# A mixer of four attentions: the memory pairs run in steps inside the stick-breaking pairs

## The chip, the cores and the metric

The kernel runs on one core of a Trainium2 chip. The metric is the time of one execution on the device, in microseconds. The median of three runs of the kernel before is 3154.68 us (3153.85 to 3159.28).

## What is computed

Two layers work on 2048 tokens of width 1024. Each layer projects its input once and feeds four groups of four heads of width 64: `fox` (causal softmax with a learned decay), `sb` (stick-breaking), `mla` (causal softmax on compressed keys and queries) and `mem` (softmax over 256 memory rows). Each group's output is multiplied by a gate, an output projection follows, and a layer norm over a scaled residual ends the layer.

```python
proj = jnp.einsum('bsd,dc->bsc', h_res, w_in[l])
# stick-breaking, for each query block; valid is key < query
z = jnp.einsum('bhqd,bhkd->bhqk', qb, k) * scale
log_keep = jnp.where(valid, jax.nn.log_sigmoid(-z), 0.0)
log_tail = lax.cumsum(log_keep, axis=3, reverse=True) - log_keep
w = jnp.where(valid, jnp.exp(jax.nn.log_sigmoid(z) + log_tail), 0.0)
out = jnp.einsum('bhqk,bhkd->bhqd', w, v)
# memory
mem_p = jax.nn.softmax(jnp.einsum('bhsd,bhmd->bhsm', mq, mk) * head_scale, axis=-1)
out_mem = jnp.einsum('bhsm,bhmd->bhsd', mem_p, mv)
# all four groups
mixed = jnp.concatenate([out_fox, out_sb, out_mla, out_mem], axis=-1)
y = jnp.einsum('bsc,cd->bsd', mixed * jax.nn.silu(gate), w_out[l])
h_res = layer_norm(DEEPNORM_ALPHA * h_res + y, ln_g[l], ln_b[l])
```

## The kernel before

Every operand of a matmul is held as two float16 numbers, a high part and the rest (`split`, `hl_tile`), and each product is three matmuls (`mm3`). Heads go in pairs: two heads fill the 128 partitions. Tokens go in four chunks of 512.

A layer runs the groups of `PLAN` one after the other: the latent projections of `mla`, then `fox0`, `fox1`, `mla0`, `mla1`, `sb0`, `sb1`, and at the end `mem0` and `mem1` together, a chunk of the one and a chunk of the other by turns. Each pair is a Python generator (`pair`). Its first part loads and splits four weight matrices (`wprep`: 8 loads, 8 maxima on VectorE, 8 casts on ScalarE, 8 splits on VectorE, line 147). A memory pair also computes its keys and values here, once. Then it yields after each of the four chunks.

A chunk of a pair first projects keys, queries, values and the gate, then works head by head. In a stick-breaking pair the work of a head comes in groups of two query tiles of 128 (`g`) and blocks of 1024 keys (`b`), last block first. One tile of a block (`stick_tile`) takes scores on TensorE (line 332), two sigmoids on ScalarE (400, 401), a backward cumulative product on VectorE (the scan, 403), a one-column scaling and a product on GpSimd (404, 405), a cast on ScalarE (411), a subtraction on VectorE (412), a transposing DMA into `pt` (354) and the matmuls with the values (859). In a memory pair a head of a chunk is one block: scores for 512 queries and 256 rows (803), maxima and a tiny scaling on VectorE (807, 808), exponentials (811), a cast (814), a subtraction on GpSimd (815), a transposing DMA and four matmuls (820). When both heads are done, `half_sum` (451, 452) gathers the halves, and an epilogue multiplies by the gate and stores (`norm_gate` with line 445, `emit_g` with 456 and 461). The epilogue of a chunk is put on the list `pending` and run by `flush` after the gate of the next chunk.

The softmax pairs (`fox`, `mla`) write logits with VectorE (369, 371), subtract on GpSimd (389) and transpose by DMA. The output projection (937) holds 8 weight tiles: four in the two `pt` tiles and four in granules; each 128-token tile `yt` is a granule too.

The order of the work comes from a list scheduler. It takes instructions in the order in which the program traces them as their priority, lets a later one go first where the earlier is not ready or has no buffer, and fixes the order of each engine's queue. All DMAs go through SP's one queue. Buffers are counted: a granule (`sbp`, 4 KB a partition, 10 of them) holds a tile of scores, of the forget rows, of `kr`, of `craw`, of `yt`, and a memory block's `pe` and `pt`; a weight place (`wp`, 4 KB, 5 of them) holds one split weight matrix. There are two `q`, two `sg`, three `hl`, five key and five value tiles.

## Time and profile before

| | |
|---|---|
| median of the runs | 3154.68 us |
| the profiled execution's own time | 3160.48 us |
| its span, first to last instruction | 3158.5 us |
| busy: TensorE, VectorE, ScalarE, GpSimd | 81%, 72%, 61%, 49% |
| mean granted TensorE clock | 0.91 |
| stick-breaking stage of layer 0, from first scan to last subtraction | 861.6 to 1306.4 us |
| output projection of layer 0 | 1443.6 to 1614.1 us |

PE is TensorE, PEld its weight loads, DVE VectorE, ACT ScalarE, POOL GpSimd, SP the engine that issues the DMAs. A duration in the trace runs from the start to the end of an instruction on its engine, so it holds what the instruction waits for once it has begun. Idle time of an engine is put down to what ended it.

### The profile page before, as it was taken

Reading aid. Unit: us, or ns where it says so; the run is one execution under the profiler, and the core shown is the slowest. Engines: PE = TensorE matmul, PEld = TensorE weight load, DVE = VectorE, ACT = ScalarE, POOL = GpSimd, SP = SyncE. Lnnn points to the kernel's source line nnn. Section 1 sums busy time; section 2 is a strip of 40 time slices with the busy share of each in tenths; the row PEclk is TensorE's granted clock in tenths of the full one; section 3 lists DMA queues with packets and bytes.
Section 4 is the critical chain, followed back from the end, with each engine's and each line's share of the span. In section 5 each row is a group of like instructions: output and inputs, shape, how many; then the busy total and the mean of one; then the engine's idle time right before and its main releaser. Section 6 shows DMA issues by size and latency. Waiting matters only on the chain. (4 is left out here: it accounts for less than half of the span.)

```text
span 3158.5 us, 47091 instructions
## 1 busy us (share of the span) xinstructions
PE 2557.1 (81%) x16412; PEld 1374.9 (44%) x16412; DVE 2280.7 (72%) x4377; ACT 1913.3 (61%) x3543; POOL 1561.7 (49%) x1079
## 2 busy tenths in 40 slices
PE   2589897888986784798978899878889768659898
PEld 2345453444553442444434545444445435334443
DVE  7756767867679989757655475577676998994565
ACT  3447667877766676474234566677767766755600
POOL 5305545555678687443210246455657867772400
PEclk9889998999998897799989999999989889769999
DMA  7748978888755745657845478897977475465752
GB/s 190 196 126 167 191 154 188 176 174 174 150 103 115 155 87 112 139 119 191 235 116 126 90 162 163 165 189 157 176 157 135 91 168 101 96 148 114 170 181 100
DMA packets 1225038, 469.46 MB, mean 149 GB/s; under 512 B 1040304, under 2 KB 1184944, under 8 KB 1224656
## 3 DMA queue, kind: packets, MB, share of 16 engines
q1 hardware_dynamic: 1224800, 466.46, 67.8%
q8 instruction: 128, 2.10, 0.3%
q14 instruction: 110, 0.90, 0.1%
HBM read 141.07 MB, written 50.53 MB: 61 GB/s over the span
## 5 line engine op out<-in xcount | busy, mean ns | idle before, releaser
L389 POOL TENSOR_TENSOR hl<-sb,hl 128x1024 f16<-128x1024 f32 (+7 forms) x384 | 609.1, 1599 | 686.3 <-ACT hl L388 503.9
L332 PE MATMUL s<-k,q 128*128 128x512 f16 (+3 forms) x1920 | 529.4, 378 | 117.7 <-ACT sg L401 34.0
L859 PE MATMUL o<-pt,v 128*128 128x256 f16 (+3 forms) x3456 | 429.4, 299 | 200.3 <-DMA pt<-hl 194.8
L405 POOL TENSOR_TENSOR sg<-sg,kp 128x127 f32<-128x127 f32 (+3 forms) x192 | 384.4, 2004 | 119.7 <-DVE kp L403 95.3
L381 ACT ACTIVATE sb<-sb,sm,sc_all 128x1024 f32<-128x1024 f32 (+7 forms) x384 | 376.5, 981 | 76.0 <-DVE sm L377 75.4
L859 PEld LDWEIGHTS <-v 128*64 128x64 f16 (+1 forms) x3456 | 245.0, 112 | 401.7 <-DMA pt<-hl 201.3
L388 ACT CAST hl<-sb 128x1024 f16<-128x1024 f32 (+7 forms) x384 | 297.7, 791 | 184.2 <-DMA pt<-hl 174.0
L937 PE MATMUL s<-wo,gc 128*128 128x512 f16 x1536 | 335.2, 381 | 0.4 <-DVE yt L941 0.4
L332 PEld LDWEIGHTS <-q 128*128 128x128 f16 x1920 | 185.2, 104 | 321.0 <-issue 201.8
L412 DVE TENSOR_TENSOR hl<-sg,hl 128x128 f16<-128x128 f32 (+3 forms) x192 | 241.9, 1267 | 44.0 <-ACT hl L411 43.0
L411 ACT CAST hl<-sg 128x128 f16<-128x128 f32 (+3 forms) x192 | 152.9, 798 | 177.5 <-DMA pt<-hl 104.4
L369 DVE CUSTOM_DVE_ANT_0 sb<-s,fb 128x512 f32<-128x512 f32 (+2 forms) x320 | 184.3, 607 | 102.9 <-DMA fb<-fds 39.6
L371 DVE TENSOR_SCALAR_CACHE_REDUCE sb<-s 128x512 f32<-128x512 f32 (+2 forms) x320 | 185.5, 606 | 72.1 <-POOL hl L389 39.8
L937 PEld LDWEIGHTS <-gc 128*128 128x128 f16 x1536 | 150.9, 98 | 182.2 <-issue 3.9
L401 ACT ACTIVATE sg<-s,sc_all 128x512 f32<-128x512 f32 (+2 forms) x320 | 199.6, 629 | 40.4 <-POOL sg L405 22.1
L403 DVE TENSOR_TENSOR_SCAN kp<-kp 128x384 f32<-128x384 f32 (+7 forms) x128 | 216.6, 1705 | 8.8 <-ACT kp L400 7.7
L400 ACT ACTIVATE kp<-s,sc_all 128x512 f32<-128x512 f32 (+2 forms) x320 | 200.0, 627 | 29.0 <-PE s L332 9.4
L276 PE MATMUL pv<-w,hT 128*128 128x128 f16 x1024 | 191.6, 227 | 24.6 <-DVE k L286 24.6
L456 POOL TENSOR_TENSOR og<-og,sg 128x512 f32<-128x512 f32 x64 | 99.2, 1550 | 223.2 <-DVE og L452 124.0
L276 PE MATMUL pg<-hT,w 128*128 128x512 f16 x512 | 197.0, 385 | 8.1 <-DVE sb L371 3.7
L277 PE MATMUL pg<-hT,w 128*128 128x512 f16 x512 | 196.3, 383 | 0.0
L278 PE MATMUL pg<-hT,w 128*128 128x512 f16 x512 | 195.9, 383 | 0.0
(238 smaller groups left out, 5930.1 us busy)
## 6 DMA issues: line engine op xcount, KB each, us to landing
raw<-in_w_in_dram SPq DMA_DIRECT2D x100, 256.0 KB, 4.7
q<-q SPq DMA_DIRECT2D x128, 128.0 KB, 2.8
fb<-fds SPq DMA_DIRECT2D x32, 512.0 KB, 4.0
gd<-gh SPq DMA_DIRECT2D x128, 128.0 KB, 2.6
raw<-in_w_out_dram SPq DMA_DIRECT2D x64, 256.0 KB, 3.8
gc<-gd SPq DMA_DIRECT2D x64, 256.0 KB, 4.0
yt<-ah SPq DMA_DIRECT2D x32, 512.0 KB, 5.3
raw<-ctd SPq DMA_DIRECT2D x48, 256.0 KB, 3.1
```

Source lines behind the costliest of these rows:

```text
L276: T.matmul(ps, lh, rh, start=(first and k == 0), stop=False)
L332: T.matmul(ps[:, :m], qs[:, h, v, j * P:(j + 1) * P], ks[c][:, h, :m], start=(v == 0), stop=last)
L381: A.activation(t, t, AF.Exp, scale=sc, bias=sm[:, j, 2:3], accum_out=su[:, b, col + j:col + j + 1])
L388: A.copy(hi, t)
L389: G.tensor_tensor(lo, t, hi, op=ALU.subtract)
L400: A.activation(keep[:, o:o + m], ps[:, :m], AF.Sigmoid, scale=nsc)
L401: A.activation(w[:, o:o + m], ps[:, :m], AF.Sigmoid, scale=sc)
L403: V.tensor_tensor_scan(keep[:, ::-1], keep[:, ::-1], keep[:, ::-1], cy, op0=ALU.mult, op1=ALU.bypass)
L405: G.tensor_tensor(w[:, :n - 1], w[:, :n - 1], keep[:, 1:n], op=ALU.mult)
L412: V.tensor_tensor(lo, w, hi, op=ALU.subtract)
L859: T.matmul(o[r0:r1, oc + j0 * P:oc + 256], vs[k // 4][:, k % 4, h, 0:r1 - r0], pcol(pt, a, k % 8, kb, j0), start=(n == 1), stop=(n == total))
L937: T.matmul(ps, gc[a][k // 4][:, k % 4, t * P:(t + 1) * P], wo[k][:, b2, n * 512:(n + 1) * 512], start=(k == 0 and a == 0 and b2 == 0), sto ...
```

## The change

`PLAN` merges each memory pair with a stick-breaking pair: `['mem0', 'sb0']`, then `['mem1', 'sb1']`. Generators now yield more often: after the gate of a chunk, after each head of a memory chunk, after each block of 1024 keys of the other kinds. `TURNS` gives the order in the merged groups: 1 is a step of the stick-breaking pair, 0 one of the memory pair. A stick-breaking chunk has 5, 5, 9 and 9 steps, a memory chunk 3. So the first two stick-breaking chunks run alone (ten steps), the third has four memory steps among it and the last has eight. Groups of one pair run through as before. Chunks of `mem` and `sb` flush their epilogue at once.

Space is moved: one more weight place, one granule less, two `og` tiles for one, one `kf` for two, and fewer small tiles under the tags of `smp`.

```diff
-PLAN = [['lat'], ['fox0'], ['fox1'], ['mla0'], ['mla1'], ['sb0'], ['sb1'], ['mem0', 'mem1']]
+PLAN = [['lat'], ['fox0'], ['fox1'], ['mla0'], ['mla1'], ['mem0', 'sb0'], ['mem1', 'sb1']]
+
+TURNS = {'mem': [1] * 10 + [1, 1, 1, 0] + [1, 1, 0] * 3 + [1] + [1, 0] * 8}
...
-    wp = pool("wp", 5)
+    wp = pool("wp", 6)
     ptp = pool("ptp", 2)
-    sbp = pool("sbp", 10)
+    sbp = pool("sbp", 9)
...
-                kf = op.tile([P, 4, 36], F32, name=nm("kf"), tag="kf", bufs=2)
+                kf = op.tile([P, 4, 36], F32, name=nm("kf"), tag="kf", bufs=1)
...
                     sg = gate_tanh(wg, u2, c, hops(c))
+                yield
 
                 flush()
-                og = op.tile([P, 512], F32, name=nm("og"), tag="og")
+                og = op.tile([P, 512], F32, name=nm("og"), tag="og", bufs=2)
...
                         half_sum(o, og, h)
+                        yield
                         continue
...
-                    half_sum(o, og, h)
+                            if (g, b) == (2 * c + 1, bs[-1]):
+                                half_sum(o, og, h)
+                            yield
...
                 pending.append(epilogue)
-                yield
+                if kind in ("mem", "sb"):
+                    flush()
...
             gens, coming = coming, None
-            for c in range(NCH):
-                if norm:
+
+            if norm:
+                for _ in range(NCH):
                     next(norm, None)
-                if c == AHEAD[gi] and gi + 1 < len(PLAN):
-                    coming = start(gi + 1)
-                for g in gens:
-                    next(g)
+                    next(gens[0])
+            turns = TURNS.get(PLAN[gi][0][:-1])
+            for g in turns or []:
+                next(gens[g], None)
+            for g in gens:
+                for _ in g:
+                    pass
```

In `smp`, the tags `am`, `at`, `ad`, `gb`, `ry`, `rt`, `mv` go from 4 tiles to 2, `wt` from 4 to 2, `sm` from 8 to 6, `cy` from 8 to 4.

## Rows read from the trace of the kernel before

**Rows 1.** Part 1 of the page: busy us (share of span) of each engine.
```profile
PE 2557.1 (81%) x16412; PEld 1374.9 (44%) x16412; DVE 2280.7 (72%) x4377; ACT 1913.3 (61%) x3543; POOL 1561.7 (49%) x1079
```

**Rows 2.** Stretches: length, then busy us of PE, PEld, DVE, ACT, POOL, clock.
```profile
862.00:1308.00 446.00, 319.66 (x2240) 179.25 (x2239) 405.97 (x410) 295.54 (x514) 335.72 (x219) 0.84 0.60 119
...
1308.00:1444.00 136.00, 122.95 (x673) 62.30 (x672) 78.50 (x154) 88.54 (x207) 47.22 (x34) 0.94 0.57 127
...
2402.00:2843.00 441.00, 322.30 (x2246) 181.78 (x2245) 406.25 (x412) 296.25 (x515) 331.81 (x219) 0.84 0.59 120
```

**Rows 3.** Stick-breaking lines, by source line: ns min/median/max, first and last start.
```profile
L403 DVE TENSOR_TENSOR_SCAN kp<-kp x64: 399/1504/3787, 861.6 to 1283.7; 128x128 f32<-128x128 f32 x8, 128x256 f32<-128x256 f32 x8, 128x384 f32<-128x384 f32 x8, 128x512 f32<-128x512 f32 x8
...
L403 DVE TENSOR_TENSOR_SCAN kp<-kp,cy x32: 2327/2345/2754, 936.4 to 1293.5; 128x1024 f32<-128x1024 f32 x32
...
L412 DVE TENSOR_TENSOR hl<-sg,hl x96: 279/1202/3044, 875.1 to 1306.4; 128x1024 f16<-128x1024 f32 x40, 128x128 f16<-128x128 f32 x8, 128x256 f16<-128x256 f32 x8, 128x384 f16<-128x384 f32 x8
...
L404 POOL TENSOR_SCALAR sg<-sg x64: 182/622/2164, 861.6 to 1284.2; 128x1 f32<-128x1 f32 x64
...
L403 DVE TENSOR_TENSOR_SCAN kp<-kp x64: 400/1504/3683, 2401.6 to 2819.9; 128x128 f32<-128x128 f32 x8, 128x256 f32<-128x256 f32 x8, 128x384 f32<-128x384 f32 x8, 128x512 f32<-128x512 f32 x8
```

**Rows 4.** Timeline of POOL and DVE from 1223: start, us, engine, line.
```profile
1223.73 6.28 POOL L405 TENSOR_TENSOR sg<-sg,kp 128x1023 f32<-128x1023 f32 x1 [2.22 <-DVE kp L403]
...
1230.21 1.99 POOL L405 TENSOR_TENSOR sg<-sg,kp 128x1023 f32<-128x1023 f32 x1
...
1228.24 1.78 DVE L121 TENSOR_SCALAR sc_all<-sc_all 128x2 f32<-128x2 f32 x1
...
1230.31 3.78 DVE L403 TENSOR_TENSOR_SCAN kp<-kp 128x896 f32<-128x896 f32 x1
```

**Rows 5.** Lines of the memory stage, layer 0: count, busy us, mean ns.
```profile
L815 POOL TENSOR_TENSOR hl<-pe,hl 128x1024 f16<-128x1024 f32 x16 | 34.0, 2128 | 47.5 <-ACT hl L814 47.4
...
L461 POOL TENSOR_TENSOR gh<-og,gh 128x256 f16<-128x256 f32 x16 | 10.7, 671 | 20.1 <-ACT gh L460 20.1
...
L456 POOL TENSOR_TENSOR og<-og,sg 128x512 f32<-128x512 f32 x8 | 10.6, 1326 | 40.5 <-DVE sg L445 35.0 <-DVE og L452 2.8 <-DVE smm L808 2.8
...
L807 DVE TENSOR_REDUCE smm<-s 128x2 f32<-128x512 f32 x32 | 21.4, 686 | 14.6 <-PE s L803 14.5
...
L286 DVE SCALAR_TENSOR_TENSOR q<-pq,q 64x512 f16<-64x512 f32 x16 | 11.0, 689 | 6.6 <-ACT q L285 6.2
...
L452 DVE TENSOR_TENSOR og<-o,og 64x512 f32<-64x512 f32 x16 | 11.0, 687 | 9.4 <-ACT og L451 9.2
...
L808 DVE TENSOR_SCALAR smm<-smm,sc_all 128x2 f32<-128x2 f32 x32 | 10.8, 344 | 0.5
...
L445 DVE TENSOR_TENSOR sg<-sg,rb 128x512 f32<-128x512 f32 x8 | 5.5, 685 | 1.1 <-PE rb L444 0.9
...
L431 DVE SCALAR_TENSOR_TENSOR sg<-sg,pg 128x512 f32<-128x512 f32 x8 | 5.5, 683 | 6.2 <-ACT sg L430 6.2
```

**Rows 6.** The memory scalings of both layers, by source line, columns as rows 3.
```profile
L808 DVE TENSOR_SCALAR smm<-smm,sc_all x64: 210/224/1678, 1335.5 to 2978.0; 128x2 f32<-128x2 f32 x64
```

**Rows 7.** The output projection's matmuls by source line, layers 0 and 1.
```profile
L937 PEld LDWEIGHTS <-gc x768: 95/98/151, 1443.6 to 1613.9; 128*128 128x128 f16 x192
...
L937 PEld LDWEIGHTS <-gc x768: 97/98/152, 2977.4 to 3149.0; 128*128 128x128 f16 x192
```

**Rows 8.** Weight splits on VectorE, by source line.
```profile
L147 DVE SCALAR_TENSOR_TENSOR w<-raw,sc_all,w x176: 234/740/2631, 47.7 to 2859.3; 128x512 f16<-128x512 f32 x104, 128x256 f16<-128x256 f32 x24, 128x128 f16<-128x128 f32 x16, 128x32 f16<-128x32 f32 x16
```

**Rows 9.** Idle time of VectorE before the logits' lines, until (us, times).
```profile
  POOL hl L389: 23.1, 17
...
  POOL hl L389: 39.8, 24
```

**Rows 10.** The stretch of fox0 in layer 0, columns as in rows 2.
```profile
236.00:395.00 159.00, 140.63 (x1042) 79.50 (x1039) 113.01 (x304) 112.39 (x195) 82.78 (x58) 0.97 0.90 179
```

**Rows 11.** Idle time before instructions on yt, layer 0's projection.
```profile
  DMA yt<-ah: 6.1, 2
```

More of the change, by code (lines that the diff above doesn't have):

```diff
@@ L41 @@
 LN_TOP = 15.0 * math.log(2.0)
-AHEAD = [9, 9, 9, 9, 9, 9, 9, 9]
 MEM_AT = 1
 SCORE_AHEAD = {"fox": 60}
-PLAN = [['lat'], ['fox0'], ['fox1'], ['mla0'], ['mla1'], ['sb0'], ['sb1'], ['mem0', 'mem1']]
+PLAN = [['lat'], ['fox0'], ['fox1'], ['mla0'], ['mla1'], ['mem0', 'sb0'], ['mem1', 'sb1']]
+TURNS = {'mem': [1] * 10 + [1, 1, 1, 0] + [1, 1, 0] * 3 + [1] + [1, 0] * 8}
 KCOF = {"fox": 0, "sb": 2, "mla": 4, "mem": 6}
@@ L130, in allmax @@
     def allmax(m, n):
-        e = smp.tile([P, 8], F32, name=nm("am"), tag="am", bufs=4)
+        e = smp.tile([P, 8], F32, name=nm("am"), tag="am", bufs=2)
         V.tensor_scalar(e[:, :n].bitcast(I32), m[:, :n].bitcast(I32), EXPM, None, op0=ALU.bitwise_and)
@@ L137, in allmax @@
         T.matmul(ps[0:n, 0:P], e.bitcast(BF16)[:, 1:2 * n:2], id_bf, start=True, stop=True)
-        t = smp.tile([8, 2], F32, name=nm("at"), tag="at", bufs=4)
+        t = smp.tile([8, 2], F32, name=nm("at"), tag="at", bufs=2)
         V.tensor_reduce(t[0:n, 0:1], ps[0:n, 0:P], axis=AX.X, op=ALU.max)
-        d = smp.tile([8, 8], BF16, name=nm("ad"), tag="ad", bufs=4)
+        d = smp.tile([8, 8], BF16, name=nm("ad"), tag="ad", bufs=2)
         V.tensor_scalar(d[0:n, 0:n], id_bf[0:n, 0:n], t[0:n, 0:1], None, op0=ALU.mult)
@@ L157, in wprep @@
         m = smp.tile([P, 8], F32, name=nm("wm"), tag="wm", bufs=4)
-        t = smp.tile([P, 2], F32, name=nm("wt"), tag="wt", bufs=4)
+        t = smp.tile([P, 2], F32, name=nm("wt"), tag="wt", bufs=2)
         raws, at = [], 0
@@ L199, in bound_gb @@
     def bound_gb(g, b, f):
-        m = smp.tile([P, 8], F32, name=nm("gb"), tag="gb", bufs=4)
+        m = smp.tile([P, 8], F32, name=nm("gb"), tag="gb", bufs=2)
         absmax(m[:, 0:1], g)
@@ L211, in rsqrt @@
     def rsqrt(v, n, pool=False):
-        y = smp.tile([P, 8], F32, name=nm("ry"), tag="ry", bufs=4)[:, :n]
-        t = smp.tile([P, 8], F32, name=nm("rt"), tag="rt", bufs=4)[:, :n]
+        y = smp.tile([P, 8], F32, name=nm("ry"), tag="ry", bufs=2)[:, :n]
+        t = smp.tile([P, 8], F32, name=nm("rt"), tag="rt", bufs=2)[:, :n]
         A.activation(y, v, AF.Sqrt)
@@ L245, in layer_norm @@
         n = len(xs)
-        mv = smp.tile([P, 2, 4], F32, name=nm("mv"), tag="mv", bufs=4)
+        mv = smp.tile([P, 2, 4], F32, name=nm("mv"), tag="mv", bufs=2)
         for t, xt in enumerate(xs):
@@ L356, in softmax_tiles @@
     def softmax_tiles(kind, h, g, qs, ks, qr, kr, fb, sc, nsc, su):
-        sm = smp.tile([P, 2, 8], F32, name=nm("sm"), tag="sm", bufs=8)
+        sm = smp.tile([P, 2, 8], F32, name=nm("sm"), tag="sm", bufs=6)
         nb = g // 4 + 1
@@ L406, in half @@
             if b:
-                ct = smp.tile([P, 8], F32, name=nm("cy"), tag="cy", bufs=8)
+                ct = smp.tile([P, 8], F32, name=nm("cy"), tag="cy", bufs=4)
                 V.tensor_copy(ct[:, 0:1], keep[:, 0:1])
```

## The prediction

> **What bounds the kernel now.** I read the page first, then a table of stretches, then the costliest instructions of the stretches that the change touches. The page gives no engine the whole time: TensorE is busy 81% and VectorE 72% [rows 1]. The stretches show why. Each layer has a stick-breaking stage followed by a memory stage. In layer 0 the first runs from the first scan at 861.6 to the last subtraction at 1306.4; the output projection's first weight load stands at 1443.6. In layer 1 the first scan is at 2401.6 and the projection begins at 2977.4 [rows 3, 7]. So the two stages cost 582.0 and 575.8 us. In the first stage VectorE is busy 406 of 446 us, GpSimd 336, TensorE 320. In the second, TensorE is busy 123 of 136, while VectorE idles 57 and GpSimd 89 [rows 2]. The stages want different engines, and the change lays one into the other.
>
> VectorE's 406 is not all work. At 1223.73 a GpSimd product starts and takes 6.28 us, where its like at 1230.21 takes 1.99. A VectorE operation on two elements, begun at 1228.24, ends with that product, 1.78 us later. A scan of 896 columns begun 0.1 us behind the second product takes 3.78 us, more than the 2.35 of a full 1024 columns [rows 3, 4]. So the two engines wait for each other on operations that read SBUF alone. I therefore add the undisturbed durations of both engines, as if they stood in one queue. Per layer there are 96 tiles: eight each of 128 to 896 columns and forty of 1024, the width of 68 full tiles. A full tile costs a scan of 2.35, a subtraction of 1.20 (L412's median) and a product of 1.99: 68 x 5.54 = 377 us. Add 96 one-column scalings of 0.18 (17), 8 gate products of 1.33 and 16 subtractions of 0.67 (21; measured in the memory stage, same shapes), and 16 weight splits of 0.74 (12) [rows 3, 4, 5, 8]. That is 427 of 446 us, 96%: this common queue bounds the stick-breaking stage.
>
> The Trainium skill, page "SBUF — State Buffer", section "Who interferes with whom", says that a VectorE instruction with two SBUF inputs and a GpSimd instruction that reads SBUF exclude each other for a whole instruction. It speaks against the change, whose GpSimd work would hide under VectorE if each engine had its own way in; the rows above agree with it. By VectorE's busy time alone the merged stage would be (406 + 62) / 0.91 = 514 us, by the rule it is the 526 worked out below.
>
> **The change, part by part.**
>
> *The memory stage goes into the stick-breaking stage.* Its instructions stay the same in number. Per layer, what joins the common queue is 16 subtractions of 2.13 (34.0), 8 gate products of 1.33 (10.6), 16 subtractions of 0.67 (10.7) and 32 tiny scalings, 0.22 undisturbed (7.0): 62 us [rows 5, 6]. The scalings' median is 0.22, their mean 0.34 and their longest 1.68; their waits for GpSimd are GpSimd's own time, which the sum has already. The rest of VectorE's share reads PSUM: 21.4 + 11.0 + 11.0 + 5.5 + 5.5 = 54 us [rows 5]. It does not join the queue and can run while GpSimd holds it. TensorE has room: 123 us are added to a stage in which it idles 126 of 446 and a new one some 80 longer.
>
> New sum: 427 + 62 = 489. Undisturbed at today's 96% that would be 509 us. I do not take that: VectorE's queue is in order, and a memory reduction that waits for its scores now holds up scans behind it. In the memory stage VectorE idles 42% [rows 2]. The ends are 96% (the stage now) and 80% (half of that idling carried in); I take 93%, near the stage's row, since 489 of the work is of its kind: 526 us.
>
> *The end of the stage.* Four of eight output weights lie in buffers that the attention blocks keep until the end. So 8 splits of 0.74 (6 us) [rows 8] and the last tile's transfer stand between the last subtraction and a full projection, where today the memory stage covers them. I take 9, between 6 and 15. Merged: 526 + 9 = 535 against 582.0 and 575.8 [rows 3, 7]: 47 and 41 us gone, 88 together.
>
> *Preparing two pairs at once.* `start` now prepares mem0 and sb0 behind mla1, and out_proj's maxima, mem1 and sb1 behind sb0. Eight more splits (6 us) and as many maxima stand before sb0's first scan. The sixth weight place lets four memory and four stick-breaking weights pass (two of the former die early). The memory keys and values take the fifth place of `kp` and `vp`, in which the next pair's first chunk is prepared ahead today. Price 0, if mla1's last chunk covers it, to 12; I take 5 a layer: +10.
>
> *Nine granules for ten.* A `fox` group of the last two chunks holds four granules, the forget rows two, the next group four: ten. `mla` needs eight and `kr`. Today VectorE waits 23.1 + 39.8 = 63 us in both layers for GpSimd to give a granule back, 1.5 at a time (41 times) [rows 9]. Below: 0, since in `fox` TensorE is busy 141 of 159 us and VectorE 113 [rows 10]. Above: two such waits more in each of the 32 large `fox` groups, all on the path: 96. I take a quarter more of today's waits, 14, as the rows of today are nearest. The projection keeps three `yt` tiles beside four weights and two rows of the norm, instead of four. Its loads are late 6.1 us in layer 0 today [rows 11]; 4 more (0 to 12), and 0 in layer 1, where a tile is given back singly.
>
> *The rest.* In layer 0 `if norm` is still true for every group, as a finished generator counts as true: mem0 and mem1 there run four steps (one chunk and a gate) ahead of their stick-breaking pair, and end half a chunk early. That moves 62 / 4 = 15 us of queue work from later chunks to earlier ones; 0, between -8 and +8. The second `og`, immediate flushes and smaller `smp` and `kf` counts: 0, each covered by work of the stage that is not at its bound; without that cover a few us. SP's queue gets the memory transposes among those of the tiles, issued in that order; in 93%.
>
> Sum against the profiled execution, 3160.5 (2 above its span): 3160.5 - 88 + 10 + 14 + 4 = 3100. The median of the runs lies 5.8 lower, so 3095.
>
> **The rivals.**
>
> *Nearly full overlap.* The stage keeps its 96%: 509 + 9 = 518, which takes 64 and 58 us: 3160.5 - 122 + 28 = 3066, or 3061 as a median; 3033 if the three costs are nothing. For it: 54 us of VectorE's new work may run while GpSimd holds the queue. Against: less room ahead.
>
> *Starved by its own places (slower).* Two `q`, two `sg` and three `hl` tiles now serve two generators: one is held by each, so neither prepares the next chunk ahead, and a late `q` stops TensorE's in-order queue at a memory score, with the scans' scores behind it. At 85% of the queue: 489 / 0.85 + 9 = 584, +2 and +8, with the costs 3160.5 + 10 + 28 = 3198, median 3192. It decides below 489 / 556 = 88%, where the gain is eaten by the 28. For it: VectorE's 57 us of idling in today's memory stage; against: several tiles of scans lie ready in granules.
>
> *The granule costs more.* With 96 in place of 14: 3182, median 3177; against no change it decides from 74 us, 2.3 for each large `fox` group. Against: TensorE and not VectorE is the busiest there.
>
> *It doesn't do what it says.* The schedule is a list by priority: memory blocks may slip behind the last tile when places are short, and the stage stays as it is with the costs added: 3188, median 3183.
>
> **How the numbers follow.** Forecast 0.55, full overlap 0.20, starved 0.13, granule 0.08, unmoved 0.04. The forecast's own range (91% to 95%, costs 15 to 40) is 3070 to 3125; with the rivals, 3035 to 3180 holds 8 in 10. A measurement of this kernel tells 0.2%, 6 us, from no change. Faster: 0.55 + 0.20, less what of the forecast lies near the break-even, 0.71; slower 0.21; the same 0.08.
>
> **What would show it.** Right: no stretch of memory scores without scans behind sb1; first scan to first projection load near 535 in each layer; VectorE's tiny scalings near 1 us beside GpSimd; `fox` and `mla` stretches longer by under 15 in both layers. Wrong: VectorE idling over 15% of the chunks with memory blocks, waiting for TensorE's scores (starved); `fox` longer by 20 or more a layer (granules); memory scores still after the last scan (unmoved).

## The result, and the profile after

The changed kernel takes 3330.27 us (median of four runs, 3325.03 to 3335.59) against 3154.26 of the kernel before in the same runs: a ratio of 1.0549, 95% interval 1.0531 to 1.0566. The forecast was 3095, with 3035 to 3180 as the range. The change costs 176 us.

The page of the kernel after, busy time of each engine, answers [rows 1]: the busy shares of all four fall, while their instructions are the same in number but for 57 on ScalarE.

```profile
PE 2596.5 (78%) x16412; PEld 1378.4 (41%) x16412; DVE 2261.5 (68%) x4377; ACT 1982.4 (60%) x3600; POOL 1520.0 (46%) x1079
```

The scans (VectorE), by source line in layer 0, and the projection's matmuls in layers 0 and 1 answer [rows 3, 7].

```profile
L404 DVE TENSOR_TENSOR_SCAN kp<-kp x64: 393/1491/3300, 915.0 to 1487.3; 128x128 f32<-128x128 f32 x8, 128x256 f32<-128x256 f32 x8, 128x384 f32<-128x384 f32 x8, 128x512 f32<-128x512 f32 x8
```
```profile
L943 PE MATMUL s<-wo,gc x768: 376/379/635, 1513.1 to 1727.7; 128*128 128x512 f16 x192
...
L943 PE MATMUL s<-wo,gc x768: 376/379/631, 3139.9 to 3313.9; 128*128 128x512 f16 x192
```

From the first scan to the first projection matmul is 598.1 us (915.0 to 1513.1), where the forecast was 535 and the kernel before takes 582.4 to its first matmul (861.6 to 1444.0). The first scan itself starts 53 us later, and the projection of layer 0 lasts 214.6 us instead of 170.1. Layer 1 has the same picture without the last point.

The stretches of layer 0 after, columns as in [rows 2]: the last logit of `mla1` to the first scan; the first stick-breaking pair; the boundary between the pairs (48th to 49th scan); the second pair; and the whole up to the end of the scans' work.

```profile
840.30:915.00 74.70, 65.19 (x459) 36.92 (x460) 40.87 (x82) 34.92 (x67) 24.21 (x17) 0.93 0.79 182
915.00:1190.00 275.00, 196.90 (x1193) 101.01 (x1192) 217.68 (x258) 186.82 (x335) 154.14 (x114) 0.84 0.48 92
1190.00:1243.00 53.00, 44.55 (x345) 28.24 (x344) 29.21 (x36) 24.72 (x49) 20.42 (x13) 0.89 0.59 116
1243.00:1497.00 254.00, 178.58 (x1110) 93.55 (x1110) 184.26 (x183) 178.28 (x323) 161.86 (x117) 0.83 0.47 93
915.00:1510.00 595.00, 423.26 (x2663) 224.50 (x2663) 439.77 (x478) 393.26 (x709) 346.43 (x248) 0.83 0.48 95
```

The first and third rows are preparation: TensorE is busy 65 of 75 and 45 of 53 us, and hardly a scan runs. In the kernel before, the row of the first kind is 13 us long, with TensorE busy all of it:

```profile
848.00:861.00 13.00, 13.00 (x85) 6.88 (x84) 2.91 (x9) 12.09 (x19) 9.49 (x6) 1.00 0.84 165
```

In the two pairs themselves VectorE is busy 79% and 73%, where the stick-breaking stage before has 91% [rows 2]. No engine is full: the last row has TensorE at 71%, VectorE at 74%, ScalarE at 66%, GpSimd at 58%.

Both layers together, after minus before, from the traces (profiled spans 3323.2 and 3158.5, 164.7 apart):

| part | forecast, us | measured, us |
|---|---|---|
| start of the layer to the first `fox` logit | 0 | -36.4 |
| `fox` and `mla` logits | +14 | +16.8 |
| last `mla` logit to first scan | +10 | +102.5 |
| first scan to projection | -88 | +34.7 |
| of that: the two pairs | | +224.8 |
| of that: boundary between the pairs | | +81.8 |
| of that: last scan to projection | | -271.8 |
| output projections | +4 | +47.0 |

The memory stage did go (-272). Its work came back in the pairs, at their boundary and ahead of them, and 137 us more with it (102.5 + 34.7).

### The profile page after: what moved, and what is told of

Read it like the earlier page. It is cut to its first block, busy times and chain, and to the rows that moved or that the text cites. A ratio compares the mean times of both kernels' runs of the same rounds, so it can differ in the third digit from the quotient of the medians.

```text
span 3323.2 us, 47109 instructions
## 1 busy us (share of the span) xinstructions
PE 2596.5 (78%) x16412; PEld 1378.4 (41%) x16412; DVE 2261.5 (68%) x4377; ACT 1982.4 (60%) x3600; POOL 1520.0 (46%) x1079
## 5 line engine op out<-in xcount | busy, mean ns | idle before, releaser
L943 PE MATMUL s<-wo,gc 128*128 128x512 f16 x1536 | 353.1, 394 | 33.1 <-DVE yt L947 22.4
L406 POOL TENSOR_TENSOR sg<-sg,kp 128x127 f32<-128x127 f32 (+3 forms) x192 | 346.2, 1804 | 61.2 <-DVE kp L404 43.5
L413 DVE TENSOR_TENSOR hl<-sg,hl 128x128 f16<-128x128 f32 (+3 forms) x192 | 233.3, 1222 | 71.6 <-ACT hl L412 70.4
L370 DVE CUSTOM_DVE_ANT_0 sb<-s,fb 128x512 f32<-128x512 f32 (+2 forms) x320 | 183.6, 606 | 109.3 <-DMA fb<-fds 41.7
L404 DVE TENSOR_TENSOR_SCAN kp<-kp 128x384 f32<-128x384 f32 (+7 forms) x128 | 206.4, 1625 | 45.0 <-ACT kp L401 44.0
L372 DVE TENSOR_SCALAR_CACHE_REDUCE sb<-s 128x512 f32<-128x512 f32 (+2 forms) x320 | 184.8, 604 | 56.4 <-POOL hl L390 32.2
L277 PE MATMUL pg<-hT,w 128*128 128x512 f16 x512 | 200.7, 392 | 8.3 <-DVE sm L370 4.3
L278 PE MATMUL pg<-hT,w 128*128 128x512 f16 x512 | 199.6, 390 | 0.0
L279 PE MATMUL pg<-hT,w 128*128 128x512 f16 x512 | 197.9, 386 | 0.3 <-DVE w L148 0.3
L277 PE MATMUL pv<-w,hT 128*128 128x128 f16 x1024 | 184.9, 223 | 11.5 <-DVE k L287 7.9
```

Source lines behind the costliest of these rows:

```text
L277: T.matmul(ps, lh, rh, start=(first and k == 0), stop=False)
L404: V.tensor_tensor_scan(keep[:, ::-1], keep[:, ::-1], keep[:, ::-1], cy, op0=ALU.mult, op1=ALU.bypass)
L406: G.tensor_tensor(w[:, :n - 1], w[:, :n - 1], keep[:, 1:n], op=ALU.mult)
L413: V.tensor_tensor(lo, w, hi, op=ALU.subtract)
L943: T.matmul(ps, gc[a][k // 4][:, k % 4, t * P:(t + 1) * P], wo[k][:, b2, n * 512:(n + 1) * 512], start=(k == 0 and a == 0 and b2 == 0), sto ...
```

## The experiments

Times are medians; the ratio is to the kernel before on the same chip, with its 95% interval. "Ahead" is from the last `mla` logit to the first scan, "stage" from the first scan to the first projection matmul (both layer 0 / layer 1), "proj" the projection of layer 0, all in us.

| kernel | time | ratio | ahead | stage | proj |
|---|---|---|---|---|---|
| before | 3154.7 | 1 | 13.5 / 13.9 | 582.4 / 576.2 | 170.1 |
| after | 3330.3 | 1.0549 [1.0531, 1.0566] | 74.7 / 55.2 | 598.1 / 595.2 | 214.6 |
| e1_space_only | 3174.2 | 1.0048 [1.0032, 1.0064] | 14.0 / 14.1 | 582.8 / 584.5 | 219.2 |
| e10_wo_in_wp | 3161.6 | 1.0013 [1.0001, 1.0025] | 14.2 / 13.6 | 586.9 / 586.2 | 169.5 |
| e12_one_wo | 3154.1 | 0.9987 [0.9977, 0.9997] | 14.0 / 12.4 | 583.8 / 577.3 | 169.9 |
| e20_wo_in_q | 3156.4 | 1.0001 [0.9992, 1.0010] | 14.1 / 12.4 | 582.7 / 580.1 | 168.6 |
| e6_in_series | 3250.9 | 1.0304 [1.0282, 1.0325] | 53.0 / 55.0 | 571.6 / 575.1 | 219.1 |
| e3_late_prep | 3259.6 | 1.0327 [1.0306, 1.0349] | 14.0 / 10.5 | 619.1 / 615.0 | 220.1 |
| e2_one_table | 3313.0 | 1.0498 [1.0482, 1.0513] | 73.3 / 54.9 | 584.8 / 588.3 | 216.8 |
| e8_own_banks | 3328.5 | 1.0543 [1.0522, 1.0564] | 14.0 / 15.0 | 647.3 / 636.4 | 223.7 |
| e9_coarse | 3242.0 | 1.0269 [1.0247, 1.0290] | 14.0 / 10.5 | 614.4 / 614.0 | 210.1 |
| e19_scores_first | 3255.6 | 1.0313 [1.0286, 1.0341] | 11.9 / 9.7 | 617.1 / 616.3 | 216.1 |
| e16_sub_on_dve | 3270.1 | 1.0354 [1.0336, 1.0372] | 14.1 / 14.9 | 623.1 / 623.3 | 218.4 |
| e18_less_port | 3241.9 | 1.0270 [1.0251, 1.0289] | 14.0 / 9.8 | 613.4 / 610.3 | 215.9 |
| e17_less_pe | 3226.4 | 1.0221 [1.0202, 1.0239] | 13.9 / 9.9 | 601.2 / 600.5 | 219.9 |
| e7_roomy | 3219.7 | 1.0198 [1.0178, 1.0219] | 41.7 / 44.8 | 606.7 / 599.5 | 178.2 |
| e14_roomy_old | 3136.0 | one run | 42.6 / 43.4 | 558.1 / 577.9 | 174.6 |
| e15_unchained | 3236.3 | one run | 37.6 / 17.0 | 615.7 / 623.5 | 181.7 |
| e21_reliefs | 3102.0 | 0.9834 [0.9806, 0.9863] | 42.6 / 44.4 | 540.9 / 538.6 | 179.2 |
| e22_mended | 3248.4 | 1.0296 [1.0279, 1.0314] | 14.0 / 14.0 | 617.4 / 624.1 | 178.1 |

**The places alone (e1).** The changed kernel's places with the order of before.

```diff
-PLAN = [..., ['mem0', 'sb0'], ['mem1', 'sb1']]
+PLAN = [..., ['sb0'], ['sb1'], ['mem0', 'mem1']]
-TURNS = {'mem': [1] * 10 + [1, 1, 1, 0] + [1, 1, 0] * 3 + [1] + [1, 0] * 8}
+TURNS = {'mem': [0, 0, 0, 1, 1, 1] * 4}
-            if norm:
+            if norm and gi == 0:
```

> The changed kernel's places (nine granules, six weight places, two og, one kf, small tags) with the order of before: sb0, sb1, then mem0 and mem1 by turns. Adding the differences of the two traces outside the merged stage: input and latent -23 and -14, fox +4 and +6, mla +10 and -4, projection +45 and +2: +26, so 3180 us. Theory that the interleaving costs the time: 3150 to 3200, well below 3330. Rival, that nine granules starve the stick-breaking stage by themselves: over 3230, with the first scan to last subtraction over 470 us (445 before).

The places cost 0.5%, some 15 us, so about 160 of the 176 us come with the order. The 15 are a balance: the projection of layer 0 is 49 us longer, and the starts of both layers are some 20 shorter each.

**No change of function table (e2).** The memory pair's exponentials and gate use the sigmoid, whose table the stick-breaking pair has loaded.

```diff
-    A.activation(pe[:, j], psv[:, j % 2], AF.Exp, scale=sc, ...
+    A.activation(pe[:, j], psv[:, j % 2], AF.Sigmoid, scale=sc, ...
-                if kind == "sb":
+                if kind in ("mem", "sb"):
                     sg = gate_sig(...)
```

> The changed kernel in which the memory pairs take a sigmoid where they took the exponential and the gate's tanh, so the function is another but count and sizes of the instructions are the same; ScalarE no longer loads a function table at each switch between a memory step and a stick-breaking step (72 loads, 15 before, 1.28 us each). Theory that the switches cost the time: 57 x 1.28 = 73 us of ScalarE, most of them on the path, 3250 to 3280. Rival, that the stage is starved of places or prepared too late: at most 20 less, 3310 or more.

ScalarE's groups of the kernel after (count, busy us, mean ns, idle time before them): 72 loads in all, where the kernel before has 15.

```profile
L813 ACT ACT_TABLE_LOAD x29 | 37.2, 1283 | 26.3 <-DVE smm L810 13.4 <-DVE cy L409 6.8 <-DVE am L136 5.8
L401 ACT ACT_TABLE_LOAD x27 | 34.6, 1283 | 0.4
```

The 57 loads more are 73 us of ScalarE. Without them (e2 has 15 again) the stages are 13.3 and 6.9 shorter and the kernel 17 us faster: a quarter of what they take is on the path.

**Memory prepared late (e3), and the two in series (e6).** In e3 the memory pair is started only after five steps of the stick-breaking pair, and layer 0's four steps of lead are gone. In e6 both are prepared ahead, and all 28 stick-breaking steps come before the memory steps.

```diff
-            for g in gens:
-                next(g)
+            for g, name in zip(gens, PLAN[gi]):
+                if name[:-1] != 'mem':
+                    next(g)
-TURNS = {'mem': [1] * 10 + [1, 1, 1, 0] + ...
+TURNS = {'mem': [1] * 5 + [0] + [1] * 5 + [1, 1, 1, 0] + ...
```
```diff
-TURNS = {'mem': [1] * 10 + [1, 1, 1, 0] + ...
+TURNS = {'mem': [1] * 28 + [0] * 12}
```

> The changed kernel, but a memory pair is prepared (weights, keys, values) only after five steps of its stick-breaking pair, and layer 0's four steps ahead are taken away; the same instructions. Between the last logits of mla and the first scan the changed kernel takes 75 and 55 us (14 and 14 before), between the 48th and 49th scan 52 and 43 (5 and 9 before). Theory that two preparations one after the other hold the stick-breaking pair back: these four fall to about 20 each, 3330 - 145 = 3185, if nothing else takes it up; over half of it: below 3260. Rival, that the memory pair takes places and time wherever it stands: 3310 or more, the gaps shorter and the pairs longer.

> The changed kernel with the same preparation of both pairs ahead, but all 28 steps of the stick-breaking pair first and then the 12 of the memory pair: no interleaving, and no four steps ahead in layer 0. Theory that preparation ahead costs the time: the gaps stay (about 180 us over before), 3155 + 26 + 100 to 180 = 3280 to 3360. Theory that the interleaving itself (tables, shared places) costs it: 3180 to 3260.

Late preparation brings the stretch ahead back to 14.0 and 10.5, and the boundary from 52.1 and 43.3 to 14.2 and 14.7. So preparing two pairs ahead is what made them long. In e6, which still prepares both ahead but has no lead, the stretch ahead of layer 0 is 53.0: the lead is 22 of the 74.7, the preparation 39. But the pairs of e3 grow by 17 to 36 us each, so the stages end 20 longer than after. The net gain is 71 us. e6, at 3250.9, is 79 faster than the changed kernel with both pairs still prepared ahead: its stages are 27 and 20 shorter, and the lead is another 22. So neither the preparation nor the taking of turns is the whole loss.

Windows of e6, columns as before, its first stick-breaking pair from first to last scan:

```profile
894.00:1092.00 198.00, 151.37 (x1002) 81.50 (x1001) 177.69 (x139) 134.04 (x236) 158.16 (x105) 0.90 0.51 91
```

A pair that runs with nothing else takes 197.4 us. Its work in the common queue is half of the prediction's terms, 188 for the full tiles and 9 for the scalings: 197. Left out on one side is its gate work, 11, and on the other some 8 of the last tiles' work, which ends behind the last scan's start; so the sum holds within a few per cent. Nine granules do not starve the pair, and the queue of VectorE and GpSimd was rightly read as its bound.

**Where the projection's time went (e10, e12, e20).** All are e1 with output weights moved out of the granules, so that `yt` has more of them: two into weight places, one (layer 0 alone) into a weight place, two into the `q` places.

```diff
-    w = granule("wo", (P, 2, D), F16)
+    w = wp.tile([P, 2, D], F16, name=nm("wo"), tag="w") if k < 6 else granule("wo", (P, 2, D), F16)
```
```diff
+    w = wp.tile([P, 2, D], ..., tag="w") if k < 5 and l == 0 else granule(...)
```
```diff
+    w = qp.tile([P, 2, D], ..., tag="q") if k < 6 else granule(...)
```

> The changed kernel's places with the order of before (3174 us), and two of the eight output weights held in weight places, which are free in the projection, instead of granules: yt has five granules for three. In layer 0 the projection takes 219 us with three (170 before with four). Theory that the third yt is what the ninth granule costs: 219 falls to 170, 3125 us, which beats the kernel before. Rival, that another place (the halved tags of the norm) holds it: 210 or more, 3170.

> The changed kernel's places with the order of before, and in layer 0 one output weight in a weight place: yt has four granules again and five of six weight places stay for the next layer's first weights. With two weights moved, the projection of layer 0 went back to 170 us, but the start of layer 1 to 148 from 128. Theory that each follows its count of places: projection 170, start of layer 1 130 to 135, 3172 - 49 + 5 = 3130, faster than before by 0.8%. Rival: the first weights of layer 1 need both places that were taken: 3155.

> The changed kernel's places with the order of before (3174 us), and two output weights held in the two q places, which nothing uses from the last pair's last scores to the next fox chunk: yt has five granules, all six weight places stay for layer 1's first weights. Theory that place counts explain both stretches: projection of layer 0 170 (219 with three yt), start of layer 1 128 (148 where weight places were taken): 3174 - 49 = 3125, 0.9% faster than before. Rival: a later q for fox0 gives it back, 3150.

Waits for `yt` in layer 0's projection after, which answers [rows 11]: 58.0 us in nine waits, 6.1 before.

```profile
  DMA yt<-ah: 58.0, 9
```

One granule more for `yt` takes the projection back to 169.9; a second adds nothing. But in all three the start of layer 1, which had fallen from 148.0 to 127.8 in e1, is back at 148, and none of the three reaches the 3125 to 3130 that was expected. The places that were taken are not the reason: in the roomy kernels below (e7, e14, e15, e21) all four output weights stay in granules, the projection takes 175 to 182, and the start is 148 to 150 too. It is short only behind a long projection. Probably the next layer's weights then had 49 us more to arrive in; no run takes that apart. The start of layer 0, 21 us shorter than before, stays.

**What the merged stage waits for.** Six variants of e3, one suspect at a time: the memory scores in the projections' PSUM banks (e8), a memory chunk's three steps together (e9), stick-breaking scores 200 ahead in priority (e19), the memory subtraction on VectorE (e16), no low half of the memory weights (e18), and three of 24 matmuls in the memory pair's query and gate projections (e17).

```diff
-    pss = [s_tile() for _ in range(2)]
+    pss = [ps_p.tile([P, 512], F32, name=nm("s"), tag="p") for _ in range(2)]
```
```diff
+TURNS = {'mem': [1] * 5 + [0] + [1] * 5 + [0] * 3 + [1] * 5 + [0] * 3 + [1] * 4 + [0] * 3 + [1] * 5 + [0] * 3 + [1] * 4}
```
```diff
+SCORE_AHEAD = {"fox": 60, "sb": 200}
```
```diff
-    G.tensor_tensor(hl[:, 1], pe, hl[:, 0], op=ALU.subtract)
+    V.tensor_tensor(hl[:, 1], pe, hl[:, 0], op=ALU.subtract)
```
```diff
-    A.copy(hl[:, 0], pe)
-    G.tensor_tensor(hl[:, 1], pe, hl[:, 0], op=ALU.subtract)
+    A.copy(hl, pe)
```
```diff
+    nk = 1 if kind == "mem" else KC
-    mm3(ps, wops(wq), hops(c))
+    mm3(ps, wops(wq)[:nk], hops(c)[:nk])
```

> The late preparation, with the memory scores in the two PSUM banks of the projections instead of two of the four that the scores share: the changed kernel's TensorE waits 30 us for stick-breaking scores until the memory exponentials give a bank back. Theory of starving, PSUM the place: first scan to projection 619 and 615 fall by 15 to 40 each. Rival (order): within 8.

> The late preparation, but a memory chunk's three steps stand together, four times in a pair (after the second chunk of the stick-breaking pair, within the third, at its end, within the last), in place of eleven single steps: a quarter of the switches between the two kinds. Theory that each switch costs (a step of the other kind waits in the queues): 619 and 615 fall by 20 or more. Theory of places: as they are, within 10.

> The late preparation with the stick-breaking scores given a priority 200 instructions ahead in the list, as fox has 60; nothing else differs. Theory of TensorE's queue: scores no longer stand behind projections, 619 and 615 fall by 15 to 40 each. Rival: within 8, as four PSUM banks and nine granules bound how far ahead scores can be.

> The late preparation with the memory blocks' subtraction on VectorE in place of GpSimd: 16 a layer, 2.13 us there, about 1.2 here by the stick-breaking subtraction of the same width. GpSimd's queue no longer stops at a memory cast, and the common access is held 15 us less a layer. Theory of waiting queues: first scan to projection 619 and 615 fall by 30 or more each. Theory of the common access alone: by 15. Rival, VectorE as the bound: up by 5 to 20.

> The late preparation without the low halves of the memory probabilities: 16 subtractions on GpSimd (34 us) and half of each memory transpose are left out a layer, the value matmuls read the high half twice. Theory that VectorE and GpSimd's common access bounds the stage: 619 and 615 fall by 30 or more each. Rival, TensorE's queue: by 12 at most.

> The late preparation in which a memory chunk's query and gate projections take 3 matmuls each instead of 24 (one of the eight slices of the input; the rest is left out): 336 matmuls of 512 columns less a layer, 0.22 us each by their spacing in the trace, 74 us of TensorE a layer. Theory that TensorE's queue holds the stage, scores standing behind projections: first scan to projection 619 and 615 fall by 40 to 70 each. Rival, the common access of VectorE and GpSimd: by 15 at most.

Against e3's stages of 619.1 and 615.0: own banks make it worse (+28, +21), which neither expectation had: the boundary is 46 long again, and why is not shown (the two banks are the projections'); coarser steps and priority hardly count (-5 and -1, -2 and +1). Taking 34 us a layer from GpSimd, with half of the transposes, gives 6 and 5; laying the subtraction on VectorE costs 4 and 8. If the queue of VectorE and GpSimd bound this stage as it bounds a pair alone, e18 would have given most of the 34. TensorE's 336 matmuls a layer less, 74 us by their spacing, give most, 18 and 15: a fifth to a quarter of what is taken away, and far from the 40 to 70 that were expected if TensorE's queue held the stage. Windows of e3 and e17 over their stages of layer 0:

```profile
849.00:1469.00 620.00, 458.44 (x2923) 248.07 (x2922) 455.19 (x562) 426.19 (x762) 359.41 (x257) 0.85 0.54 110
```
```profile
840.00:1441.00 601.00, 405.14 (x2596) 223.27 (x2597) 458.13 (x560) 423.10 (x756) 368.75 (x258) 0.79 0.56 113
```

The second window holds 327 matmuls less, but only 53 us less of busy time. The granted clock falls from 0.85 to 0.79 with the lighter TensorE, between the levels of 1.2 and 2.4 GHz, so it stood at the lower one for more of the stretch. That takes part of the relief back; how much, no run here tells.

**Room, and the chain of waits (e7, e14, e15).** The low half of the layer's input is left out. That frees space for thirteen granules, five `hl`, three `q` and three `sg` (e7: late order; e14: order of before). In e15 (eleven granules, four `hl`) the memory blocks' operations read constant tiles, so hardly one waits for the one before it.

```diff
-    qp = pool("qp", 2)
+    qp = pool("qp", 3)
-    sbp = pool("sbp", 9)
-    phl = pool("phl", 3)
-    gp = pool("gp", 2)
+    sbp = pool("sbp", 13)
+    phl = pool("phl", 5)
+    gp = pool("gp", 3)
```
```diff
-    V.tensor_reduce(sm[:, 2 * u:2 * u + 2], psv, axis=AX.X, op=ALU.max)
+    V.tensor_reduce(sm[:, 2 * u:2 * u + 2], c_pe[:, 0:2], axis=AX.X, op=ALU.max)
...
-    A.copy(hl[:, 0], pe)
+    A.copy(hl[:, 0], c_pe)
```

> The late preparation, with the low halves of the layer's input left out (each matmul that reads one reads the high half in its place, so count and size of the matmuls stay), which frees 32 KB of a partition: 13 granules for 9, five hl for three, three q and three sg for two. From the first scan to the projection the late preparation takes 619 and 615 us, the kernel before 582 and 576. Theory that the interleaved stage is starved of places: 540 or less in each layer. Rival, that steps of two pairs in each engine's one queue, in a fixed order, hold each other up however many places there are: 590 or more.

> The order of before with the ample places of the roomy kernel (low halves of the layer's input left out, 13 granules, five hl, three q, three sg). Control for it: from first scan to projection the merged roomy kernel takes 607 and 600 us. Theory that merging by turns costs time by itself: 560 to 585 here, below the merged one with the same places. Rival, that the ample places changed the stage in both: 595 or more.

> The roomy merged kernel (11 granules, four hl) in which the memory blocks' reductions, exponentials, casts, subtractions and value matmuls read constant tiles, in place of each other's results: every instruction stays in number, size and engine, but none of them waits for the one before, and what they compute is lost. The scheduler is free to put them earlier, so I count from mla's last logits to the projection: 648 and 644 us in the roomy kernel. Theory that the memory chain's waits in in-order queues cost the time: under 590. Rival, that the occupied time on VectorE, GpSimd and their common access costs it: over 630.

With room the merged stages are 12 and 15 shorter, no more. And with the same room the order of before takes 558.1 and 577.9: merging costs 49 and 22 us even where places are plenty. Taking the chain away changes nothing that counts: from the last `mla` logit to the projection it is 653.2 and 640.6, against 648.3 and 644.3 in e7. The comparison is not clean, as e15 has two granules and one `hl` less, and its reductions read SBUF in place of PSUM (21 us a layer that the prediction would put into the common queue). By an estimate from these rows that could hide some 30 us, not the 58 that the theory asked for.

Yet the chain is plain to see in the trace. A timeline of the kernel after, all engines (start, us, engine, line; in brackets the idle time before and what ended it):

```profile
1120.05 2.72 DVE L404 TENSOR_TENSOR_SCAN kp<-kp 128x1024 f32<-128x1024 f32 x1
...
1122.69 0.66 DVE L809 TENSOR_REDUCE smm<-s 128x2 f32<-128x512 f32 x1
...
1123.91 2.04 DVE L810 TENSOR_SCALAR smm<-smm,sc_all 128x2 f32<-128x2 f32 x1
1123.93 1.99 POOL L406 TENSOR_TENSOR sg<-sg,kp 128x1023 f32<-128x1023 f32 x1
...
1125.93 0.21 DVE L810 TENSOR_SCALAR smm<-smm,sc_all 128x2 f32<-128x2 f32 x1
1126.03 1.28 ACT L813 ACT_TABLE_LOAD   x1 [4.44 <-DVE cy L409]
...
1127.33 0.56 ACT L813 ACTIVATE pe<-s,smm,sc_all 128x256 f32<-128x256 f32 x1
...
1128.58 1.01 PE L333 MATMUL s<-k,q 128*128 128x512 f16 x2 [6.91 <-ACT pe L813]
...
1134.71 0.41 ACT L461 CAST gh<-og 128x256 f16<-128x256 f32 x1
...
1135.14 1.28 ACT L401 ACT_TABLE_LOAD   x1
...
1136.44 0.69 ACT L401 ACTIVATE kp<-s,sc_all 128x512 f32<-128x512 f32 x1
...
1141.68 2.34 DVE L404 TENSOR_TENSOR_SCAN kp<-kp,cy 128x1024 f32<-128x1024 f32 x1
```

A two-element scaling takes 2.04 us where its median is 0.23: a GpSimd product of 1.99 starts 0.02 behind it, and both end together. The exponentials stand behind the scaling, the next stick-breaking scores wait 6.91 us behind the exponentials for a PSUM tile, and between two scans lie 19 us. The lesson of e15 is that a chain of waits in a timeline is not yet a cause: without this one the stage was as long. What took its place in e15 was not followed up.

**All reliefs at once (e21), and the two mends at once (e22).** e21 is e7 with e2's single table, e17's fewer matmuls and e18's missing low half. e22 is e3 with e20's two `q` places.

```diff
# e21
-    sg = gate_sig(wg, u_g8[:, kc:kc + 1], c, hops(c))
+    sg = gate_sig(wg, u_g8[:, kc:kc + 1], c, hops(c)[:1] if kind == "mem" else hops(c))
...
# e22
-    w = granule("wo", (P, 2, D), F16)
+    w = qp.tile([P, 2, D], F16, name=nm("wo"), tag="q") if k < 6 else granule("wo", (P, 2, D), F16)
```

> Late preparation as before, and four reliefs of the memory pair at once: the low half of the layer's input is left out (thirteen granules, five hl, three q and sg), one function table for everything, 3 of 24 matmuls for the memory pair's query and gate projections, and no low half of the memory weights (no GpSimd subtraction, half the transposes). Each alone changed first scan to projection (619.1 and 615.0 in the kernel that only prepares late) by -12 and -15, about -13 and -7, -18 and -15, -6 and -5. Theory that the queues of all four engines hold each other up, each with its share: the reliefs add, 570 and 573. Rival, one hidden cause that each relief only touched: no better than the best alone, about 600. Rival, the common queue of VectorE and GpSimd as forecast, with the stalls gone once room is there: its work is now 489 - 34 = 455, at 93% 489, and 9 for the end: 498.

> Late preparation, and two of layer 0's and layer 1's output weights in the two q places instead of granules, so that the projection has five granules for yt. Theory that the two costs are separate: projection of layer 0 at 170 in place of 220 (-50), start of layer 1 back from 125 to 148 (+23), the rest as with late preparation alone (merged stages 619 and 615): 3259.6 - 27 = 3233, ratio 1.025. Rival, the weights that now wait for the last q of the merged stage delay the projection: the stage's end 10 later in each layer and 3253. In neither case is the kernel before reached, since the merged stages alone cost 37 and 39 more.

e21's window over its stage in layer 0:

```profile
841.00:1382.00 541.00, 384.77 (x2525) 208.22 (x2525) 449.10 (x542) 371.47 (x711) 320.53 (x236) 0.83 0.55 112
```

One by one the four reliefs give 12.4 + 13.3 + 17.9 + 5.7 = 49 us in layer 0 and 42 in layer 1 (the 13.3 against the changed kernel, the others against e3). Together they give 78 and 76. So they more than add. That also holds from the last `mla` logit on, which is the fairer count, since room lets more work slip in between that logit and the first scan (42 us against 14): singly 23 and 9, together 50 and 42. None of the three expectations is met: 541 lies between the 570 of reliefs that add and the 498 of a common queue without stalls, and one hidden cause was to leave 600. That speaks against the common queue as the bound, too: with 455 us of work left in it, the stage takes 541, 84% of it. The forecast's 535 is nearly reached, but only with a good part of the memory work left out. Whether the order of before would gain as much from the same omissions was not run, so this ratio says nothing for the merge.

e22 shows what mending the two clear losses leaves: 3248.4. The `q` places give the projection 42 of its 50 us back, the start of layer 1 returns to 147.5, and its stage gets 9 longer (layer 0's does not), which brings the time near the rival's 3253 and not the 3233. No kernel here that does the whole work beats the one before by more than the 0.2% that can be told: the best, e12, is at 0.9987. e22's span is 88 above that of before: 35.0 and 47.9 of it lie in the two stages.

## Why the prediction was wrong, step by step

**The bound of the kernel before** was right. A stick-breaking pair alone runs in the time of its common queue (e6, 197.4 us for 197, within a few per cent).

**"I take 93%, near the stage's row, since 489 of the work is of its kind"** is the step that failed. It carried the occupancy of a stage with one chain of work over to a stage with two. The queue's 489 us take 598 after and 619 in e3, 82% and 79%. The sum had a price for VectorE's and GpSimd's instructions and none for ScalarE's or TensorE's queue, each of which now holds both chains' work in one order. TensorE was called room, since it idles 126 of 446 us, and ScalarE has no term at all; in e3 they are busy 458 and 426 of 620 us. e17, e2 and e21 show that such room is not free. The wait of VectorE that grew most is that of the scans for ScalarE's sigmoids. The kernel before, 862 to 1308, and after, 915 to 1510 (waiting engine and line, what ended the wait: us, times, longest us):

```profile
DVE kp L403 <- ACT kp L400: 4.0, 7, 1.7
```
```profile
DVE kp L404 <- ACT kp L401: 34.6, 23, 3.7
...
DVE smm L809 <- PE s L805: 4.9, 5, 2.3
```

The "starved" rival had the direction and 584 for the stage, and its sign, VectorE idle over 15%, came (21% and 27% of the pairs). But VectorE waits for ScalarE there and hardly for TensorE's scores, and the places to which the rival put it are worth 12 and 15 us a layer (e7).

**"Preparing two pairs at once, +10"** was off by 92 us ahead of the first scans, and by another 82 at the boundaries. The prediction counted eight splits and eight maxima of VectorE, and not what they hold back. The memory pair's weights are prepared first, so those of the stick-breaking pair are ready late. In layer 1 the last split of the sixteen begins at 2519.6, 30 us behind the last `mla` logit; before, the last of the eight begins at 2351.6, 36 us ahead of it.

```profile
L148 DVE SCALAR_TENSOR_TENSOR w<-raw,sc_all,w x16: 734/1020/2604, 2419.7 to 2519.6; 128x512 f16<-128x512 f32 x16
```
```profile
L147 DVE SCALAR_TENSOR_TENSOR w<-raw,sc_all,w x8: 745/746/752, 2318.9 to 2351.6; 128x512 f16<-128x512 f32 x8
```

So the stick-breaking pair's own projections, most of which ran between `mla1`'s last scores before, now follow behind them. Of the 43 us that TensorE is busy in layer 1's stretch of 55.2, 28 are these projections and 6 the memory pair's keys and values. In layer 0 the four steps ahead add the memory pair's queries, gate and scores to that: 32 of the 65 busy us are the memory pair's. Preparing it later saves 71 us of the whole (e3), and lengthens the pairs by 17 to 36 each.

**"Layer 0's four memory steps ahead, 0"** is 22 us (74.7 against 53.0 in e6).

**"The projection, +4"** is +44.5 in layer 0. The term was raised from today's late loads, 6.1 us, as if one tile fewer made each a bit later. With three `yt` tiles, of which the layer norm takes two at a time, the waits for a load come nine times, 58 us. The end of the range, 12, was too near the row of before. The shorter starts, 36 us over both layers, were not foreseen.

**"Nine granules, +14"** came near by luck: `fox` is 10.9 and `mla` 5.9 us longer over both layers, but not for the reason given. In e1, with the same nine granules, `fox` is 6.6 longer and `mla` 8.3 shorter, -2 in all. And the waits for GpSimd to give a granule back, from which the term was worked out, did not grow: 27.7 and 32.2 us, against 23.1 and 39.8 [rows 9]. They are listed for the kernel after by line, over both layers (us, times), the `fox` line and the `mla` line:

```profile
  POOL hl L390: 27.7, 11
```
```profile
  POOL hl L390: 32.2, 22
```

And fox0 in layer 0 keeps the engines as busy as in [rows 10], so TensorE stays the busiest there:

```profile
214.00:373.00 159.00, 141.93 (x1083) 82.02 (x1083) 96.99 (x286) 108.33 (x191) 80.79 (x56) 0.97 0.83 172
```

**"The scalings near 1 us beside GpSimd"** as a sign: by line over both layers after, against [rows 6], the median stays 0.23, and the longest grows from 1.68 to 2.04. It was a poor sign, for one late scaling holds up ScalarE and TensorE at once.

```profile
L810 DVE TENSOR_SCALAR smm<-smm,sc_all x64: 197/228/2041, 882.1 to 3136.1; 128x2 f32<-128x2 f32 x64
```

**Function tables** were not in the sum at all; they are worth 17 us of the 176.

The terms miss by 123 (stage), 92 (ahead), 43 (projection), 3 (logits) and -36 (starts): 225, the distance from the -60 forecast for the span to the +165 measured.

What stays open: how the 37 and 39 us by which e3's stages exceed those of before divide among the engines. The reliefs name TensorE, the tables, places and GpSimd as parts and show that they depend on each other; no run takes one queue's order apart from its work. One rival was hardly tried, the queue of SP, through which all DMAs go in one order. TensorE's longest wait in layer 0's merged stage is for transposed tiles, 87.6 us of 595, against 62.1 of 446 in the stick-breaking stage before. And the stores of the gated outputs, which are issued among the transposes, keep that queue waiting for GpSimd 79.4 us there, 27.8 in the two stages before. e18 makes the memory transposes smaller, but not fewer.

```profile
PE o L859 <- DMA pt<-hl: 62.1, 19, 7.8
```
```profile
PE o L862 <- DMA pt<-hl: 87.6, 31, 9.8
```
```profile
SPq L463 <- POOL gh L462: 79.4, 16, 10.6
```

## What to carry to other kernels

Before two stages that want different engines are merged, price the new stage by each engine's queue, and do not take over the occupancy that one chain alone reached. When something is prepared ahead, ask which work it pushes back, here the projections of the pair that comes first, which lost their cover. And treat the last buffer of a rotating set as a step, not as a slope.

## What the hardware showed beside that

A table load takes 1283 ns in every row, and 57 of them cost 17 us of time, 0.30 each. The Trainium skill, "ScalarE: Activation LUTs", section "What ACT_TABLE_LOAD costs", gives 2.66 us a switch with its drain. An estimate by that figure is 152 us of ScalarE's time. The trace here shows no drain: in the timeline above a cast ends at 1135.12, the load begins at 1135.14, and the sigmoid at 1136.44.

Places count in `mla`: with thirteen granules and five `hl`, its logits take 253.7 and 258.5 us (e14), where nine or ten granules and three `hl` give 292 to 306. VectorE's waits for GpSimd before those logits fall from 39.8 us [rows 9] to 1.2 in e14, over both layers:

```profile
  POOL hl L390: 1.2, 1
```

Some 30 us a layer of that come back as a longer stretch ahead of the first scan (42.6 and 43.4 against 13.5 and 13.9). Which of the two places it is, no run tells, and the space for them was had here only by leaving data out.
